# A hybrid decoder block on one Trainium2 core: two PSUM accumulation banks in place of four

## Chip, core and metric

The kernel runs on one core of one Trainium2 chip. The metric is the device time of one execution in microseconds (us), taken as the median of several runs. Profiles are of one execution, taken by the hardware profiler.

## What is computed

One decoder layer over 16 meta tokens and 256 input tokens (272 rows of 1024 numbers), in float32. Cut to what matters:

```
a = rmsnorm(h, g_mix);  proj = a @ w_in            # split into q k v qi ki wi cu cb cc ga gb
y_attn = sparse_attention(q, k, v, qi, ki, wi) @ w_attn_out     # 8 heads, best 68 keys per query
y_conv = (cb * conv3(cc * cu)) @ w_conv_out
h = h + (sigmoid(ga) * y_attn + sigmoid(gb) * y_conv) @ w_out
f = rmsnorm(h, g_ffn)
h = h + (silu(f @ w_gate) * (f @ w_up)) @ w_down   # width 2816
out = rmsnorm(h, g_final)[16:]
```

## The kernel before, in words

**Units.** All weights are cut into 158 tiles of 128 x 1024 numbers, listed in `UNITS` (`unit_order`, lines 49 to 63). A tile holds, for 128 output columns, the eight blocks of 128 x 128 that contract with the 1024 inputs. A unit is the work of one such tile: eight steps of three float32r products each (high weight times high activation, high times low, low times high), summed in one PSUM bank. `narrow` (line 218) writes 24 matmuls of 256 to 272 columns (lines 214 to 216). `product` (line 255) takes the high and the low activation side by side in one matmul of 512 columns (line 250) and adds one of 256 columns for the low weight (line 253), so its bank holds two halves that `total` (line 243) adds up, with a copy on ACT (line 245) and an addition on DVE (line 246).

**Order of the units.** Four `qi`, three early gates, `ki`; then for eight blocks `cc`, `cu`, `cb`; for eight heads `k`, `q`, `v`; then gates, `co` and `ao` (output projections of the two branches), `wo`, and 22 pairs `gate`, `up` of the FFN. The down projection has eight long sums of 22 blocks each. The order is written out by hand (`manual_schedule`): every engine works through its instructions in the order in which the program issues them.

**What stands around a unit.** `step` (line 434) first calls `ahead(i)`, which issues the splitting of coming weights: ACT rounds a tile to its high part (line 137), DVE subtracts to get the low part (line 145), and SP fetches the next tile into a ring of seven. `ahead` ends with `flush`, which issues the DVE subtractions put off by `split` (lines 118 to 124): the low half of an activation. After that come the unit's matmuls, and then the instructions that read its bank. So a subtraction that `split` puts off reaches DVE only in the next unit's call.

**Heads.** Right behind the matmuls of unit `k`, `behind(j, 0)` issues the attention of head j-2 (`attend`, lines 427 to 431), the logits and softmax of head j-1 (`logits`) and the transposes of v of head j-1 (`values`). Then `split` copies k to its high part on ACT and puts off `k_lo` (line 120), which reads the same bank. Unit `q` follows, then unit `v`.

**Start.** The first units are issued by hand (lines 574 to 601): after each unit's matmuls the one before it is read, by `indexer_queries` (ACT line 294, DVE line 296) or `early_gate` (DVE line 571), behind one or two weight splits. Between them the row sums are turned into inverse norms on POOL (line 201), spread by transposes (line 207) and applied (ACT, POOL and DVE lines 564 to 566). `ki` is read by `indexer_keys` (last at line 281).

**FFN.** The first `gate` unit's bank is kept until the inverse norms `rstd` are there: its `total` is issued behind `final_rms`, the first `up` unit and the copy of `rstd`. `final_rms` (line 625) multiplies the squares with a column of ones (line 191), which gives row sums in two banks.

**Banks.** PSUM has two pools: `acc` for the units (`bank`, line 88) and `misc` for all else (`side`, line 91), four banks each, handed out in rotation. A unit's first matmul waits until the last reader of the bank's former tile has ended.

Of the kernel before, what the change touches and what calls it, by code (L numbers as in the profile page):

```python
# [68 lines left out]
def program(nc, tc, h_in, params, weights, out):  # L69
    ctx = ExitStack()  # L70
# [5 lines left out]
    raws = pool("raws", RAW)  # L76
    his = pool("his", HIS)
    los = pool("los", LOS)
    acc = ctx.enter_context(tc.tile_pool(name="acc", bufs=4, space=bass.MemoryType.PSUM))
    misc = ctx.enter_context(tc.tile_pool(name="misc", bufs=4, space=bass.MemoryType.PSUM))  # L80
    ctx.enter_context(tc.manual_schedule())

# [35 lines left out]
    def split(hi, lo, src, now=False):  # L118
        act(hi, src, AF.Copy)  # L119
        low = lambda: V.tensor_sub(lo, src, hi.bitcast(F32))  # L120
        if now:
            low()
        else:
            pending.append(low)
# [25 lines left out]
    def ahead(i):  # L150
        split_to(i + 1 + AHEAD)
        high_to(i + 2 + AHEAD)
        flush()
# [31 lines left out]
    B = [(0, P), (P, P)]  # L185

    def token_sums(parts, groups, where=bank):
        o = [where() for _ in groups]
        for i, sq in enumerate(parts):
            for t, (c0, n) in enumerate(groups):  # L190
                mm(o[t][0:n, 0:1], sq[:, c0:c0 + n], ones, start=i == 0, stop=i == len(parts) - 1)
        return o

    def inverse_rms(o, groups):
        r = ring.tile([P, 3], F32, name="rt")
        if len(groups) == 3:
            V.memset(r[:, 0:1], 1.0)
        for t, (c0, n) in enumerate(groups):
            V.tensor_scalar(r[0:n, t:t + 1], o[t][0:n, 0:1], 1.0 / D, EPS, op0=OP.mult, op1=OP.add)
        r = r[:, 0:len(groups)]  # L200
        G.tensor_tensor(r, r, half[:, 0:len(groups)], OP.pow)  # L201
        return r

    def spread(r, groups):
        o = side()
        for i, (c0, n) in enumerate(groups):
            nc.tensor.transpose(o[:, c0:c0 + n], r[0:n, i:i + 1].to_broadcast([n, P]), ident[0:n, 0:n])
        return o
# [34 lines left out]
    def total(o):  # L243
        t = temp(S)
        act(t, o[:, S:2 * S], AF.Copy)  # L245
        V.tensor_tensor(t, o[:, 0:S], t, OP.add)  # L246
        return t
# [7 lines left out]
    def product(i, src, c0=0):  # L255
        o = bank()
        hi, lo = got.pop(i)
        w = lambda k: slice(k * P, k * P + P)
        for k in range(KT - 1):
            wide_high(o, hi[:, w(k)], src, k, c0, start=k == 0, stop=False)  # L260
            wide_low(o, lo[:, w(k)], src, k, c0, start=False, stop=False)
        k = KT - 1
        wide_low(o, lo[:, w(k)], src, k, c0, start=False, stop=False)
        wide_high(o, hi[:, w(k)], src, k, c0, start=False, stop=True)
        return o
# [321 lines left out]
    r = inverse_rms(token_sums(sums, ALL, side), ALL)  # L587
# [25 lines left out]
    sq_sum = one.tile([P, S], F32, name="sq_sum")  # L613

    def squares(j, h):
        if j == 0:
            act(sq_sum, h, AF.Square)
        else:
            sq = temp(S)
            act(sq, h, AF.Square)  # L620
            if j == KT - 1:
                return sq
            G.tensor_tensor(sq_sum, sq_sum, sq, OP.add)  # L623

    def final_rms():
        return inverse_rms(token_sums([sq_sum, sq_last], B), B)

    for j in range(KT):
        i = first["wo"] + j
# [9 lines left out]
        sq_last = squares(j, h)  # L639
# [4 lines left out]
    for j in range(NF):  # L644
        i = first["gate"] + 2 * j
        ahead(i)
        og = product(i, fT)
        if j == 0:
            r = final_rms()
            ahead(i + 1)  # L650
            ou = product(i + 1, fT)
            act(rstd, spread(r, B)[:, 0:S], AF.Copy)
        s = total(og)
        V.tensor_tensor(s, s, rstd, OP.mult)
        act(s, s, AF.Silu)  # L655
        G.tensor_tensor(s, s, rstd, OP.mult)  # L656
        if j:
            ahead(i + 1)
            ou = product(i + 1, fT)
        V.tensor_tensor(s, s, total(ou), OP.mult)  # L660
        split(gu[j // KT].hi[:, j % KT], gu[j // KT].lo[:, j % KT], s)

    for j in range(KT):
# [21 lines left out]
        sq_last = squares(j, h)  # L685
# [3 lines left out]
    def turn_out(k):  # L689
        for t in range(2):  # L690
            c = (k % 4) * P
            nc.tensor.transpose(tps[t][k // 4][:, c:c + P], hT[:, k, t * P:t * P + P], ident)

    for k in range(4):
        turn_out(k)
    r = final_rms()
    for k in range(4, KT):
        turn_out(k)
    y_out = one.tile([P, 2, D], F32, name="big0")
# [56 lines left out]
```

## Time and profile before

| what | value |
|---|---|
| median of 3 runs | 504.36 us (504.21 to 505.34) |
| profiled execution, span from first to last instruction | 502.3 us |
| profiled execution, its own time besides the span | not given |
| TensorE (PE) busy | 492.7 us, 98% |
| weight loads (PEld) | 444.5 us, 88% |
| VectorE (DVE) busy | 362.7 us, 72% |
| ScalarE (ACT) busy | 301.9 us, 60% |
| GpSimd (POOL) busy | 73.3 us, 15% |
| DMA, weights queue | 51.6% of 16 engines |

The engines' busy times are shares of the same span and overlap. The start of an instruction and its duration give its end; "[idle before <-releaser]" behind a row is how long the engine stood idle before it and which instruction ended that.

### The profile page before, as it was taken

The numbers are of one execution on the slowest core, as the hardware profiler recorded it, in microseconds if no ns is written. First come the engines' busy times: TensorE is split into PE (matmuls) and PEld (weight loads), VectorE is DVE, ScalarE is ACT, GpSimd is POOL, SyncE is SP. The second block draws the span as 40 slices with busy tenths as digits, with TensorE's granted clock in tenths as the row PEclk, the third lists the DMA queues.
The fourth block names the chain that finished last, engine by engine and source line by source line (L and its number), as shares of the span: only waits on it lengthen the run. The fifth ranks groups of instructions, "written<-read, shape, count | busy, mean of one in ns | idle before, by whom it ended". The sixth has DMA issues, their size and how long they took to land.

```text
span 502.3 us, 8349 instructions
## 1 busy us (share of the span) xinstructions
PE 492.7 (98%) x3157; PEld 444.5 (88%) x3157; DVE 362.7 (72%) x661; ACT 301.9 (60%) x567; POOL 73.3 (15%) x75
## 2 busy tenths in 40 slices
PE   8999999999999999999999999999999999999995
PEld 6988889999999999888888989888888888888895
DVE  5898678886677777587776797778777777764521
ACT  6685566655577777765656465666666656553511
POOL 3451112211000000000000012121221122000110
PEclk9999999999999999999999999999999999999999
DMA  8847335556434544365556475456656565665002
GB/s 311 322 129 251 127 127 185 193 169 215 163 127 127 159 135 133 124 204 197 182 176 201 133 246 176 155 187 201 203 178 197 173 196 182 206 204 177 1 0 85
DMA packets 24376, 86.09 MB, mean 171 GB/s; under 512 B 2832, under 2 KB 2832, under 8 KB 24336
## 3 DMA queue, kind: packets, MB, share of 16 engines
q1 hardware_dynamic: 24192, 85.54, 51.6%
q8 instruction: 25, 0.41, 0.3%
q14 instruction: 15, 0.12, 0.1%
q10 hardware_dynamic: 144, 0.02, 0.0%
HBM read 84.50 MB, written 1.05 MB: 170 GB/s over the span
## 4 chain that ended last, share of the span: by engine, by line
PE 90%; issue 3%; DVE 2%; ACT 1%; DMA 1%; POOL 1%; SPq 0%; POOLq 0%; DVEq 0%
PE acc L250 42%; PE acc L253 21%; PE acc L214 7%; PE acc L215 7%; PE acc L216 7%; DMA h_all<-in_h_in_dram 1%; PE misc L304 1%; DVE aT L566 1%; PE misc L303 1%; PE misc L410 1%; ACT temp L555 0%; PE misc L427 0%; PE misc L216 0%; POOL rt L201 0%; PE misc L214 0%
## 5 line engine op out<-in xcount | busy, mean ns | idle before, releaser
L250 PE MATMUL acc<-aT,whi 128*128 128x512 f32 x576 | 202.7, 399 | 0.0
L145 DVE TENSOR_TENSOR wlo<-raw,whi 128x1024 fp32r<-128x1024 f32 x158 | 192.8, 1225 | 7.0 <-ACT whi L137 4.8
L137 ACT ACTIVATE whi<-raw 128x1024 fp32r<-128x1024 f32 x158 | 163.8, 1047 | 0.4 <-PE acc L250 0.3
L253 PE MATMUL acc<-aT,wlo 128*128 128x256 f32 x576 | 150.1, 281 | 0.0
L250 PEld LDWEIGHTS acc<-aT,whi 128*128 128x128 f32 x576 | 105.3, 188 | 19.7
L250 PE MATMUL acc<-big,whi 128*128 128x512 f32 x330 | 115.2, 394 | 0.0
L253 PEld LDWEIGHTS acc<-aT,wlo 128*128 128x128 f32 x576 | 108.8, 189 | 5.7
L253 PE MATMUL acc<-big,wlo 128*128 128x256 f32 x330 | 88.4, 282 | 0.0
L215 PE MATMUL acc<-aT,whi 128*128 128x272 f32 (+2 forms) x272 | 78.1, 287 | 1.1 <-DVE aT L566 1.1
L214 PE MATMUL acc<-aT,whi 128*128 128x272 f32 (+2 forms) x272 | 78.6, 289 | 0.0
L216 PE MATMUL acc<-aT,wlo 128*128 128x272 f32 (+2 forms) x272 | 77.6, 285 | 0.0
L246 DVE TENSOR_TENSOR temp<-acc,temp 128x256 f32<-128x256 f32 x87 | 36.9, 424 | 49.8 <-ACT temp L245 49.8
L250 PEld LDWEIGHTS acc<-big,whi 128*128 128x128 f32 x330 | 60.6, 188 | 11.9
L253 PEld LDWEIGHTS acc<-big,wlo 128*128 128x128 f32 x330 | 62.0, 188 | 2.5
L215 PEld LDWEIGHTS acc<-aT,whi 128*128 128x128 f32 x272 | 51.3, 189 | 1.8 <-DVE aT L566 1.3
L214 PEld LDWEIGHTS acc<-aT,whi 128*128 128x128 f32 x272 | 51.4, 189 | 0.7
L216 PEld LDWEIGHTS acc<-aT,wlo 128*128 128x128 f32 x272 | 51.2, 188 | 0.0
L119 ACT ACTIVATE big<-temp 128x256 fp32r<-128x256 f32 x45 | 18.8, 418 | 47.0 <-DVE temp L660 23.2
L623 POOL TENSOR_TENSOR sq_sum<-sq_sum,temp 128x256 f32<-128x256 f32 x12 | 11.0, 918 | 236.6 <-ACT temp L620 236.6
L245 ACT ACTIVATE temp<-acc 128x256 f32<-128x256 f32 x87 | 32.7, 376 | 13.9 <-PE acc L250 11.5
L656 POOL TENSOR_TENSOR temp<-temp,rstd 128x256 f32<-128x256 f32 x22 | 26.0, 1182 | 93.9 <-ACT temp L655 93.9
L239 DVE TENSOR_TENSOR h_all<-h_all,acc 128x256 f32<-128x256 f32 x16 | 6.7, 416 | 28.6 <-PE acc L250 21.7
(162 smaller groups left out, 529.5 us busy)
## 6 DMA issues: line engine op xcount, KB each, us to landing
raw<-in_weights_dram SPq DMA_DIRECT2D x158, 512.0 KB, 3.5
h_all<-in_h_in_dram SPq DMA_DIRECT2D x4, 272.0 KB, 4.6
out_dram<-big SPq DMA_DIRECT2D x4, 256.0 KB, 2.3
raw<-in_weights_dram SPq DMA_DIRECT2D x2, 256.0 KB, 3.8
par<-in_params_dram ACTq DMA_DIRECT2D x1, 24.0 KB, 3.3
```

What stands on the lines that cost most here:

```text
L119: act(hi, src, AF.Copy)
L137: act(high[i], raw[i], AF.Copy)
L145: V.tensor_sub(lo, raw.pop(i), high[i].bitcast(F32))
L214: mm(o, wh, xh, start=first, stop=False)
L215: mm(o, wh, xl, start=False, stop=False)
L216: mm(o, wl, xh, start=False, stop=last)
L245: act(t, o[:, S:2 * S], AF.Copy)
L246: V.tensor_tensor(t, o[:, 0:S], t, OP.add)
L250: mm(halves(o), w, src.both[:, k, :, c0:c0 + S], **kw)
L253: mm(o[:, 0:S], w, src.hi[:, k, c0:c0 + S], **kw)
L623: G.tensor_tensor(sq_sum, sq_sum, sq, OP.add)
L656: G.tensor_tensor(s, s, rstd, OP.mult)
```

## The change

The pool `acc` gets two banks instead of four. The two row sums of the FFN take banks from `misc` (`side`), because the first gate's bank is still held when they are made; the last row sums keep the main banks, because all four side banks hold transposes by then.

```diff
-    acc = ctx.enter_context(tc.tile_pool(name="acc", bufs=4, space=bass.MemoryType.PSUM))
+    acc = ctx.enter_context(tc.tile_pool(name="acc", bufs=2, space=bass.MemoryType.PSUM))
...
-    def final_rms():
-        return inverse_rms(token_sums([sq_sum, sq_last], B), B)
+    def final_rms(where):
+        return inverse_rms(token_sums([sq_sum, sq_last], B, where), B)
...
         if j == 0:
-            r = final_rms()
+            r = final_rms(side)
...
     for k in range(4):
         turn_out(k)
-    r = final_rms()
+    r = final_rms(bank)
```

No instruction changes its place on any engine; the tiles' banks and the waits at the units' first matmuls change. On TensorE, at the end of a head's unit `q` and the start of its unit `v`, whose first matmul is the row of line 214 (the third to last of these rows; "waits" names the engines whose counters it waits for):

```order
 L253 MATMUL acc<-aT,wlo 128x256 x2
 L250 MATMUL acc<-aT,whi 128x512
-L214 MATMUL acc<-aT,whi 128x272
+L214 MATMUL acc<-aT,whi 128x272 [waits DVE_49]
 L215 MATMUL acc<-aT,whi 128x272
 L216 MATMUL acc<-aT,wlo 128x272
```

The first matmul of `v` waited for nothing before; now it waits for DVE. The reader it waits for stands in this part of DVE's queue, which is the same in both kernels, here for head 7 (`acc_2541` is the bank of its unit `k`, `misc_2566` the attention of head 5, `misc_2576` the logits and `misc_2591` the values of head 6):

```order
L246 TENSOR_TENSOR temp_2572<-misc_2566,temp_2572 128x256 [waits Activation_49]
L377 ISA p_2583,mx_2584<-misc_2576,bias_121 128x144 [waits PE_49]
L377 ISA mx_2584 128x1
L377 ISA p_2583,mx_2584<-misc_2576,bias_121 128x272
L377 ISA mx_2584 128x1
L378 TENSOR_SCALAR mx_2584<-mx_2584 128x2 [waits DVE_49]
L145 TENSOR_TENSOR wlo_2603<-raw_2233,whi_2537 128x1024 [waits DMAHW0_49]
L120 TENSOR_TENSOR big1_1816<-temp_2572,big1_1816 128x256 [waits Activation_49]
L120 TENSOR_TENSOR v_lo_2596<-misc_2591,v_hi_2595 128x256 [waits PE_49,Activation_49]
L403 TENSOR_TENSOR vm0_479<-misc_2591,vm0_479 16x128
L120 TENSOR_TENSOR k_lo_2601<-acc_2541,k_hi_2600 128x272 [waits Activation_49]
```

Nothing moved here: `k_lo` still stands last of eleven rows that begin with the attention issued behind unit `k`. On TensorE at the FFN's second gate (`acc_3893`; `acc_3854` is the first `up`, `misc_3871` the spread inverse norms), before:

```order
L250 MATMUL acc_3854<-aT_3566,whi_3689 128x512
L207 MATMUL misc_3871<-ident_114,rt_3844 128x128 [waits Pool_49]
L207 MATMUL misc_3871<-ident_114,rt_3844 128x128 [waits DVE_49]
L250 MATMUL acc_3893<-aT_3566,whi_3719 128x512
L253 MATMUL acc_3893<-aT_3566,wlo_3745 128x256
```

and with the change:

```order
L250 MATMUL acc_3854<-aT_3566,whi_3689 128x512
L207 MATMUL misc_3871<-ident_114,rt_3844 128x128 [waits Pool_49]
L207 MATMUL misc_3871<-ident_114,rt_3844 128x128 [waits DVE_49]
L250 MATMUL acc_3893<-aT_3566,whi_3719 128x512 [waits DVE_49,PE_49]
L253 MATMUL acc_3893<-aT_3566,wlo_3745 128x256
```

The second gate's first matmul, which waited for nothing, now waits for DVE, which reads the first gate's bank.

## Rows read from the trace of the kernel before

**Rows 1.** Page, busy us (share of the span) x instructions:

```profile
PE 492.7 (98%) x3157; PEld 444.5 (88%) x3157; DVE 362.7 (72%) x661; ACT 301.9 (60%) x567; POOL 73.3 (15%) x75
```

**Rows 2.** Page, chain that ended last, share of the span by engine:

```profile
PE 90%; issue 3%; DVE 2%; ACT 1%; DMA 1%; POOL 1%; SPq 0%; POOLq 0%; DVEq 0%
```

**Rows 3.** TensorE's waits, longest first: us in total, times, longest:

```profile
PE acc L182 <- POOL temp L156: 1.1, 1, 1.1
```

**Rows 4.** Stretches: us, busy us (instructions) by engine, granted clock, DMA share, GB/s:

```profile
30.00:42.00 12.00, 10.91 (x88) 10.46 (x86) 11.91 (x19) 8.24 (x12) 1.79 (x2) 1.00 0.61 194
...
118.00:206.00 88.00, 88.00 (x657) 84.29 (x657) 63.42 (x151) 60.18 (x142) 0.00 (x0) 1.00 0.47 150
...
320.00:490.00 170.00, 170.00 (x978) 148.67 (x977) 115.77 (x177) 93.47 (x155) 31.77 (x27) 1.00 0.51 164
```

**Rows 5.** Timeline of PE, 18 to 39 us: start us, duration us, instruction, [idle before]:

```profile
18.69 0.37 PE L214 MATMUL acc<-big,whi 128*128 128x256 f32 x1
...
22.21 0.59 PE L207 MATMUL misc<-ident,rt 16*128 16x16 f32 x3 [0.40 <-POOL rt L201]
...
31.18 0.29 PE L214 MATMUL acc<-aT,whi 128*128 128x272 f32 x1
31.31 0.29 PE L215 MATMUL acc<-aT,whi 128*128 128x272 f32 x1
...
34.44 0.39 PE L215 MATMUL acc<-aT,whi 128*128 128x272 f32 x1 [1.09 <-DVE aT L566]
34.67 0.30 PE L216 MATMUL acc<-aT,wlo 128*128 128x272 f32 x1
...
38.49 0.28 PE L214 MATMUL acc<-aT,whi 128*128 128x258 f32 x1
```

**Rows 6.** Timeline of DVE, 18 to 40 us:

```profile
18.93 0.86 DVE L296 TENSOR_TENSOR big<-acc,big 64x256 fp32r<-64x256 f32 x2
...
33.56 0.41 DVE L571 TENSOR_TENSOR gate<-acc,rstd 128x256 f32<-128x256 f32 x1
...
39.75 0.42 DVE L281 SCALAR_TENSOR_TENSOR temp<-acc,rstd 8x256 f32<-8x256 f32 x1
```

**Rows 7.** Timeline of POOL, 20 us:

```profile
20.26 1.90 POOL L201 TENSOR_TENSOR rt<-rt,half 128x3 f32<-128x3 f32 x1 [4.47 <-DVE rt L199]
```

**Rows 8.** Timeline of PE: first matmuls of v (heads 0, 1, 7), ga1, gates 1, 2:

```profile
119.96 0.29 PE L214 MATMUL acc<-aT,whi 128*128 128x272 f32 x1
...
129.80 0.29 PE L214 MATMUL acc<-aT,whi 128*128 128x272 f32 x1
...
196.34 0.29 PE L214 MATMUL acc<-aT,whi 128*128 128x272 f32 x1
...
210.04 0.40 PE L250 MATMUL acc<-aT,whi 128*128 128x512 f32 x1
...
313.47 0.48 PE L250 MATMUL acc<-aT,whi 128*128 128x512 f32 x1
...
318.96 0.63 PE L250 MATMUL acc<-aT,whi 128*128 128x512 f32 x2
```

**Rows 9.** Timeline of DVE: last readers of the banks two units ahead:

```profile
119.68 0.43 DVE L120 TENSOR_TENSOR k_lo<-acc,k_hi 128x272 fp32r<-128x272 f32 x1
...
130.28 0.44 DVE L120 TENSOR_TENSOR k_lo<-acc,k_hi 128x272 fp32r<-128x272 f32 x1
...
193.12 0.42 DVE L246 TENSOR_TENSOR temp<-misc,temp 128x256 f32<-128x256 f32 x1 [2.34 <-ACT temp L245]
...
196.86 0.44 DVE L120 TENSOR_TENSOR k_lo<-acc,k_hi 128x272 fp32r<-128x272 f32 x1
...
210.62 0.42 DVE L246 TENSOR_TENSOR temp<-acc,temp 128x256 f32<-128x256 f32 x1
...
314.44 0.43 DVE L246 TENSOR_TENSOR temp<-acc,temp 128x256 f32<-128x256 f32 x1 [2.54 <-ACT temp L245]
...
319.46 0.42 DVE L246 TENSOR_TENSOR temp<-acc,temp 128x256 f32<-128x256 f32 x1 [0.23 <-ACT temp L245]
```

## The prediction

> **What bounds the kernel now.** I read the busy times first: TensorE is busy for 492.7 us of a span of 502.3 us [rows 1], and the chain of work that ended last is TensorE for 90% [rows 2]. Next the list of TensorE's waits: it has five lines of one wait each, the longest 1.1 us, together 3.7 us, all before 35 us [rows 3, 5]. From 118 to 206 us, the attention stage, TensorE is busy for 88.00 of 88.00 us, and from 320 to 490 us for 170.00 of 170.00, at the full granted clock [rows 4]. So TensorE's stream is the time: whatever makes it wait after 42 us is added whole, because no gap behind it can take the delay back. The other engines run beside it, and their lag is free as long as nobody on TensorE waits for it. That lag is what the change puts a price on.
>
> **The change part by part.** Matmuls, copies and transfers stay as many and in the same order on each queue, SP's and POOL's too. Only two things move: which bank a tile gets, and so what a unit's first matmul waits for. With two banks, unit n needs the last reader of unit n-2. I went through all units of the trace and compared the start of each unit's first matmul with the end of the last read of the unit two ahead. Most have 1 to 2.5 us to spare. Where the reader ends later, the difference is the price. Two small amounts come on top. The release takes about 0.05 us: POOL's power ends at 22.16 us and the transpose that needs it starts at 22.21 [rows 5, 7]. And the restart costs about 0.1 us: without a wait the second matmul of a unit starts 0.13 us after the first (31.18 and 31.31), after the existing wait at 34.44 it starts 0.23 us after it (34.67) [rows 5], since the weights could not be loaded ahead.
>
> *Start, up to 42 us.* The indexer queries qi1 and qi3 meet first. qi3's first matmul starts at 18.69 [rows 5]; qi1's last reader, the second of two DVE subtractions, ends at 18.93 + 0.86 = 19.79 [rows 6]. qi3 starts 1.15 us later, 1.25 with the restart. The transposes of the row norms at 22.21 now wait 0.40 us for POOL [rows 5], which absorbs that much, so they and all of the norm's consumers on ACT, POOL and DVE shift by some 0.8 us. With that shift the unit ki has to wait for the gate unit two ahead: 33.56 + 0.41 + 0.8 + 0.05 = 34.8 against 31.18 [rows 5, 6], 3.7 us late. Inside ki the wait of 1.1 us for aT goes away [rows 5], leaving some 2.6. The next meeting, cu0 with ki, agrees: its last reader ends at 39.75 + 0.42 + 0.8 + 0.05 = 41.0 against 38.49 [rows 5, 6], 2.5 late, 2.6 with the restart. I take **2.6 us**; the ends are 1.7 (the readers do not shift at all: 40.22 - 38.49) and 3.8 (nothing is absorbed).
>
> *Attention.* Units run k, q, v for each head, so v waits for k's bank. k is read twice: by ACT, and by a DVE subtraction that is queued until the q unit's call, behind the previous head's softmax work, a weight split, and v's two subtractions. For head 7 that subtraction ends at 196.86 + 0.44 = 197.30, and v's first matmul starts at 196.34; for head 1 it is 130.72 against 129.80 [rows 8, 9]. With release: 1.01 and 0.97 us. Heads 2 to 6 lie between 0.98 and 1.06. Does it repeat, or does the first wait buy the rest? It repeats: the DVE run ahead of k_lo begins each time with an idle of 2.34 us [rows 9], so DVE is not behind; it waits for the matmuls that stand right behind k, and a later k makes it later by as much. Seven times (1.01 + 0.1) is 7.8 us. Head 0 has no such work: 119.68 + 0.43 + 0.05 against 119.96 is 0.2, with restart 0.3 [rows 8, 9]. **8.1 us**; ends 7.2 (no restart cost) and 9.4 (each wait of heads 1 to 7 longer by 0.2 us, half the subtraction's own 0.44).
>
> *First gates.* ga1 waits for gb0, whose sum ends on DVE at 210.62 + 0.42 = 211.04; ga1 starts at 210.04 [rows 8, 9]: 1.05 plus the restart, **1.15 us**. co0 just ahead waits for ga0 by a part of the same time and adds nothing beyond it.
>
> *FFN, row sums.* Four matmuls of one column and two DVE reads change their bank only: nothing. But the first gate's result is held until the row norms are there: its sum ends at 314.44 + 0.43 = 314.87, and gate 1 starts at 313.47 [rows 8, 9]: 1.45 plus 0.1, **1.55 us**. In the units that follow the readers are late too: gate 1 is read until 319.46 + 0.42 = 319.88, while gate 2 starts at 319.59 - 0.40 = 319.19 [rows 8, 9], the rows' end less one matmul. That is 0.69 late, but the 1.55 us already lost put gate 2 behind it, if the readers' backlog stays where it is. If it moves with TensorE, 2 us more are due here: that is the upper end.
>
> *Everything else* has time to spare: the projections of the convolution stage, the output projections (a reader at the closest ends 0.6 us early) and the down projection, where a bank is held for 8 us. The last row sums use the two main banks, whose readers must have finished anyway for the sums to exist: nothing.
>
> Sum: 2.6 + 8.1 + 1.15 + 1.55 = 13.4 us. The profiled span of 502.3 becomes 515.7. The page gives no time of that execution besides its span; the runs' median is 504.36, 2.1 us above it, and I carry these 2.1 over: **517.8 us**. Measurements of this kernel tell 0.2% (1 us) from no change, as its runs spread from 504.21 to 505.34.
>
> **The clock.** TensorE has paused here before without losing its clock: around the 1.1 us wait at 34 us the granted clock is 1.00, the 2.4 GHz level, for the whole stretch from 30 to 42 us [rows 4, 5]. The Trainium skill, "TensorE: Matmul & The Clock Gate", section "A second HAM failure mode: psum-queue depth-cycling", tells of a kernel that cycled through PSUM banks, paused often between groups of matmuls and kept falling to the lower clock. By that rule the pauses of the attention stage would each cost more than themselves. The row speaks against it; as a rival it gets a price below.
>
> **The rivals.**
> *The backlog moves along (FFN).* Gate 1's delay shifts ACT and DVE as well, and the next units wait again, 0.7 us and falling. For it: each unit's readers start from its own last matmul. Against: the backlog comes from one table load and the norms, which the delay does not repeat. 519.8 us.
> *Part of the waits is absorbed.* If k_lo's DVE work moves forward once TensorE stalls (weight splits ahead of it done earlier), the heads fall from 1.1 to some 0.5 us: 4 us less, 513.8. Against: the idle of 2.34 us ahead of that work [rows 9].
> *The clock falls.* If each v unit of seven heads ran at 1.2 GHz, each would take its 24 spacings of 0.13 us twice, 3.1 us more: 517.8 + 21.8 = 539.6. The row at 34 us is against it. By the rule of the Trainium skill above it would be this case.
> *Not slower.* The lost 13 us come back in the FFN if the supply of weights sets the pace there: while TensorE waits, the DMA and the splits would run up to seven tiles ahead, and later units would run faster. It decides from the point at which 66 units could each give back 0.2 us. Then 504.4. Against it: TensorE shows no wait at all after 35 us and is busy 170.00 of 170.00 us [rows 3, 4]; a full stream has nothing to give back.
> *The change does nothing.* If no unit's start were tied to the last reader of the unit two ahead, 504.4 too. The order of the built kernel shows those waits where there were none.
>
> **How the numbers follow.** Forecast as summed 0.74; backlog moving 0.11; partly absorbed 0.09; clock 0.03; not slower 0.02; nothing done 0.01. The forecast's own ends are 1.7 + 7.2 + 1.05 + 1.45 = 11.4, so 515.8, and 3.8 + 9.4 + 1.2 + 3.6 = 18.0, so 522.4, if all err the same way. The range of 515.0 to 521.0 takes in the low end, the moving backlog and most of the high end. It leaves out the clock, no change, and the lower part of the absorbed case. Slower by over 0.2%: all cases but the last two, 0.97. These two make 0.03, of which I give 0.02 to within 0.2% and 0.01 to faster, since stages that get weights early could only gain by small amounts.
>
> **What would show it.** In the changed kernel's list of TensorE's waits there should be new lines: for k_lo eight times, about 1.0 us each and 0.2 for head 0; for the sum at L246 at ga1, co0 and gate 1, together some 2.6; for L296, L571 and L281 before 45 us. TensorE's busy time stays near 492 us while the span grows, the attention stage from 88 to some 96 us, the stage of 320 to 490 us keeps its length, and the granted clock stays 1.00. Wrong would be: attention waits that shrink from head to head, a stage at a lower clock, or waits that go on through the FFN.

## The result, and the profile after

The changed kernel takes 518.38 us (median of 4 runs, 517.72 to 518.66). The kernel before, run beside it on the same chip, takes 504.85 us (4 runs, 504.21 to 505.34). The ratio is 1.027, with a 95% interval of 1.0252 to 1.0288. The profiled execution took 517.72 us and has a span of 515.9 us, 13.6 us more than the span before.

The page of the changed kernel, busy time by engine and the chain that ended last by engine, to be read beside [rows 1, 2]:

```profile
PE 496.9 (96%) x3157; PEld 444.9 (86%) x3157; DVE 363.9 (71%) x661; ACT 303.2 (59%) x567; POOL 73.3 (14%) x75
```

```profile
PE 83%; DVE 6%; ACT 5%; issue 3%; DMA 1%; SPq 0%; POOL 0%; POOLq 0%; DVEq 0%; ACTq 0%
```

Every engine does as many instructions as before, in nearly the same busy time. What is new is that the chain leaves TensorE: DVE and ACT have 11% of it, where they had 3%. The waits of TensorE in the changed kernel (us in total, times, longest) say which work of theirs it is:

```profile
PE acc L214 <- DVE k_lo L120: 6.1, 7, 0.9
PE acc L250 <- DVE temp L246: 1.9, 2, 1.3
PE acc L214 <- DVE big L296: 1.5, 2, 1.3
PE acc L227 <- DVE big L546: 1.2, 1, 1.2
PE acc L182 <- POOL temp L156: 1.1, 1, 1.1
PE acc L214 <- DVE gate L571: 1.0, 2, 0.8
PE acc L214 <- DVE rt L197: 0.2, 1, 0.2
```

The lines for L546 and L182 wait for data and not for a bank (the wait for POOL is that of [rows 3]). The others are the forecast waits: `k_lo` in the heads, the sum at L246 at the gates, and L296 and L571 at the start; L197 is a memset of 0.06 us right behind a read at L296. Two forecast lines are missing, L281 and an eighth `k_lo`: cu0 and v0 do start later, but TensorE's records of the matmuls ahead of them cover the 0.2 to 0.3 us.

Busy time by stage, with borders shifted by the delay so far, so that each stretch holds the same work as before (us, then busy us and instructions of PE, PEld, DVE, ACT, POOL, then the granted clock, DMA share and GB/s):

```profile
44.56:120.56 76.00, 76.00 (x527) 69.61 (x527) 60.04 (x135) 46.53 (x91) 17.33 (x18) 1.00 0.49 163
120.56:217.05 96.49, 90.33 (x658) 84.43 (x657) 64.12 (x151) 60.25 (x142) 0.00 (x0) 1.00 0.42 137
...
333.65:503.65 170.00, 170.00 (x978) 148.60 (x977) 114.29 (x175) 93.29 (x154) 31.12 (x27) 1.00 0.49 161
```

The convolution stage and the FFN hold the matmuls of before in the same time, 170.00 us for the FFN as in [rows 4]. The attention stage needs 96.49 us for what took 88.00 us [rows 4]; 0.08 of them are a late second matmul of cu0, which the shift of 2.56 us leaves out. Of the 8.41 us that are left TensorE stands idle for 6.16 us. The other 2.25 us, some 0.3 at each of the eight waits, count as busy: a matmul is recorded with 0.29 us although the next one usually starts 0.13 us after it [rows 5], so the last one before a wait covers part of it, and the first one behind it is drawn out.

TensorE's rows at the places of the forecast (start us, duration us, instruction, idle before): qi3, the transposes, ki and cu0 of the start; v0, v1 with its second matmul, v7; co0, ga1, gate 1:

```profile
19.96 0.36 PE L214 MATMUL acc<-big,whi 128*128 128x256 f32 x1 [0.17 <-DVE rt L197]
...
22.98 0.59 PE L207 MATMUL misc<-ident,rt 16*128 16x16 f32 x3
...
34.85 0.36 PE L214 MATMUL acc<-aT,whi 128*128 128x272 f32 x1 [0.21 <-DVE gate L571]
...
41.05 0.36 PE L214 MATMUL acc<-aT,whi 128*128 128x258 f32 x1
...
122.79 0.39 PE L214 MATMUL acc<-aT,whi 128*128 128x272 f32 x1
...
133.75 0.39 PE L214 MATMUL acc<-aT,whi 128*128 128x272 f32 x1 [0.83 <-DVE k_lo L120]
133.98 0.29 PE L215 MATMUL acc<-aT,whi 128*128 128x272 f32 x1
...
207.29 0.39 PE L214 MATMUL acc<-aT,whi 128*128 128x272 f32 x1 [0.87 <-DVE k_lo L120]
...
219.04 0.47 PE L250 MATMUL acc<-big,whi 128*128 128x512 f32 x1 [0.58 <-DVE temp L246]
...
222.16 0.50 PE L250 MATMUL acc<-aT,whi 128*128 128x512 f32 x1
...
327.13 0.47 PE L250 MATMUL acc<-aT,whi 128*128 128x512 f32 x1 [1.30 <-DVE temp L246]
```

And the readers that they wait for, on DVE:

```profile
18.96 0.86 DVE L296 TENSOR_TENSOR big<-acc,big 64x256 fp32r<-64x256 f32 x2
...
40.49 0.42 DVE L281 SCALAR_TENSOR_TENSOR temp<-acc,rstd 8x256 f32<-8x256 f32 x1
...
133.26 0.44 DVE L120 TENSOR_TENSOR k_lo<-acc,k_hi 128x272 fp32r<-128x272 f32 x1
...
203.04 0.42 DVE L246 TENSOR_TENSOR temp<-misc,temp 128x256 f32<-128x256 f32 x1 [2.70 <-ACT temp L245]
...
206.80 0.44 DVE L120 TENSOR_TENSOR k_lo<-acc,k_hi 128x272 fp32r<-128x272 f32 x1
...
326.56 0.42 DVE L246 TENSOR_TENSOR temp<-acc,temp 128x256 f32<-128x256 f32 x1 [2.54 <-ACT temp L245]
...
331.58 0.42 DVE L246 TENSOR_TENSOR temp<-acc,temp 128x256 f32<-128x256 f32 x1 [0.23 <-ACT temp L245]
```

Laid against the rows of before, these give the delay of TensorE from place to place:

| place | start before, us [rows 5, 8] | start after, us | delay, us |
|---|---|---|---|
| cu0 | 38.49 | 41.05 | 2.56 |
| v0 | 119.96 | 122.79 | 2.83 |
| v1 | 129.80 | 133.75 | 3.95 |
| v7 | 196.34 | 207.29 | 10.95 |
| ga1 | 210.04 | 222.16 | 12.12 |
| gate 1 | 313.47 | 327.13 | 13.66 |

From v1 to v7 each head adds 7.00 / 6 = 1.17 us, and nothing is added behind gate 1. The table is read at first matmuls. Where the second one comes late too (the restart), 0.08 us follow at cu0 and some 0.1 at each v and at ga1; the 0.1 of ga1 is gone again at 229 us, in the last products of the attention.

### The profile page after: what moved, and what is told of

The parts are those of the page before. It is cut to its first block, busy times and chain, and to the rows that moved or that the text cites. A ratio compares the mean times of both kernels' runs of the same rounds, so it can differ in the third digit from the quotient of the medians.

```text
span 515.9 us, 8360 instructions
## 1 busy us (share of the span) xinstructions
PE 496.9 (96%) x3157; PEld 444.9 (86%) x3157; DVE 363.9 (71%) x661; ACT 303.2 (59%) x567; POOL 73.3 (14%) x75
## 4 chain that ended last, share of the span: by engine, by line
PE 83%; DVE 6%; ACT 5%; issue 3%; DMA 1%; SPq 0%; POOL 0%; POOLq 0%; DVEq 0%; ACTq 0%
PE acc L250 38%; PE acc L253 19%; PE acc L214 8%; PE acc L215 7%; PE acc L216 7%; ACT p L381 1%; DMA h_all<-in_h_in_dram 1%; DVE p L377 1%; PE misc L304 1%; DVE temp L246 1%; DVE wlo L145 1%; ACT whi L137 1%; DVE aT L566 1%; ACT temp L245 1%; DVE v_lo L120 1%
## 5 line engine op out<-in xcount | busy, mean ns | idle before, releaser
L246 DVE TENSOR_TENSOR temp<-acc,temp 128x256 f32<-128x256 f32 x87 | 36.9, 424 | 52.4 <-ACT temp L245 52.4
```

## The experiments

**Late readers** is the theory of the prediction: a unit's first matmul waits for the last read of the unit two ahead, and each wait costs the lag of that read and a restart of some 0.1 us. **Shared depth** is the first rival: the smaller number of banks costs time in itself, spread over the units, so that each bank taken away costs a part and an earlier read helps little. **Slower stream** is the second: matmuls or reads run slower in the changed banks, the row sums' side banks among them.

**Three banks.** One number of the changed kernel:

```diff
-    acc = ctx.enter_context(tc.tile_pool(name="acc", bufs=2, space=bass.MemoryType.PSUM))
+    acc = ctx.enter_context(tc.tile_pool(name="acc", bufs=3, space=bass.MemoryType.PSUM))
```

> The changed kernel with three accumulation banks instead of two, all else as changed. Late readers (my theory): a unit waits for the last reader of the unit three ahead. In the trace of before no such reader ends later than the first matmul it would hold, by at least 0.3 us, so all of the 13.4 to 13.7 us comes back: 504.4 to 505.5 us, and TensorE's wait list is that of before. Shared depth (rival: ACT and DVE run behind, and each bank less costs in proportion): about half of the loss stays, some 511 us. Slower stream (rival: matmuls run slower when fewer banks alternate): between the two, with TensorE's mean matmul times above those of before.

Measured: 504.08 us (10 runs) beside 504.39 (13 runs), ratio 0.9994 (0.9985 to 1.0003). TensorE's waits are five lines, all before 42 us, and none is for a bank. So the time does not fall bank by bank. With three banks a unit waits for the read three ahead, which has a whole unit more, 24 matmuls of 0.125 us [rows 5]; a reader 1 us late is then 2 us early. This speaks against shared depth.

**Row sums in side banks, four main banks.** The change's second part alone, which also stands in the three kernels further down that keep four banks:

```diff
         if j == 0:
-            r = final_rms()
+            r = final_rms(side)
```

> Four accumulation banks as before, and only the FFN's row sums moved to side banks, the other part of the change done alone. My theory: no effect, a span of 502.3 us within 0.5 us. Rival: the row sums in side banks hold up the transposes behind them, which take side banks too: the first FFN units up to 1 us later.

Measured: 504.91 us in one run, span 503.1 us, and no new wait of TensorE. The 0.8 us over the profile of before arise at 10 to 13 us, far ahead of the row sums, where TensorE's clock fell in this execution (the last section): it is 0.84 us late at 23 us and still so at the end. The row sums cost nothing.

**k read first, two banks.** In the changed kernel, the copy and the subtraction of k are issued ahead of the attention of the head before, and the subtraction is not put off:

```diff
             o = narrow(i, aT)
-            behind(j, 0)
             k = Pair(two, [P, L], "k")
-            split(k.hi, k.lo, o)
+            split(k.hi, k.lo, o, now=True)
+            behind(j, 0)
```

> The changed kernel (two banks), with unit k's two readers (the copy on ACT and the subtraction on DVE) issued right behind k's matmuls, ahead of the attention, logits and values of the heads before, and the subtraction not put off. Late readers: the eight waits of unit v for k_lo vanish, 8.5 us of the 13.7: a span of 507.4 us and 509.9 us in time; the waits at the start, at the first gates and at the FFN stay as they are. Shared depth: v's wait is replaced by waits of q, v or k for other readers in the same stage, and under 3 us come back: 515 us or more.

Measured: 509.01 us (4 runs, 508.63 to 509.5), ratio to the kernel before 1.0092 (1.0075 to 1.0109); span 506.8 us. All waits for `k_lo` are gone, and the attention stage (us and columns as in the stages above) holds its 657 matmuls in the former time:

```profile
120.50:208.50 88.00, 88.00 (x657) 84.20 (x656) 63.55 (x150) 60.92 (x143) 0.00 (x0) 1.00 0.45 150
```

All of the attention stage's 8.4 us come back from the order of k's reads, with two banks. The time is 0.9 us below the forecast of 509.9, of which 0.55 us lie at the start, which the edit does not touch (cu0 came 2.02 us later than before, not 2.56). This is the strongest evidence for late readers, and the one that shared depth and a slower stream cannot give. A slower stream is also refuted by the changed kernel itself, whose 978 matmuls of the FFN take 170.00 us with two banks as with four.

**First FFN gate read first, two banks.** The sum of the first gate is issued ahead of the row norms, not behind them:

```diff
         og = product(i, fT)
+        s = total(og)
...
-        s = total(og)
```

> The changed kernel (two banks), with the first FFN gate's sum issued right behind its matmuls, ahead of the row norms. Late readers: the wait of gate 1, 1.4 us, vanishes. The readers of the next units, 0.7 us late in the trace of before, are then met for the first time, less the 0.4 us that the earlier sum takes off ACT's and DVE's queues: gate 2 waits some 0.3 to 0.5 us, and the span becomes 514.9 us. If the readers' backlog were only a matter of that one sum, the full 1.4 us come back: 514.5 us. Shared depth: the waits of the next units together take all of it back: 515.9 us.

Measured: 517.25 us in one run, span 515.5 us. Gate 1's delay of 1.54 us is gone, and two small ones take its place, 0.37 us at the up unit behind it and 0.19 at gate 2, so some 1.0 us is saved, as expected. The span hides it, because in this execution TensorE's clock fell at 11 us and the start ended 0.6 us later.

**Start's reads first, two banks.** In the start, each read is issued ahead of the weight splits that stood before it (four such places):

```diff
-    split_to(3)
     indexer_queries(last, 0)
+    split_to(3)
...
-        split_to(i + 3)
...
             early_gate(last, i - 1)
+        split_to(i + 3)
```

> The changed kernel (two banks), with the readers of the first units (indexer queries and early gates) issued ahead of the weight splits that stood before them, at the start only. Late readers: the waits of qi2, qi3 and of the gate units and ki for those readers vanish or shrink, and 1.5 to 2.6 us of the start's 2.6 come back: the matmuls of cu0 start 0 to 1.1 us later than before instead of 2.6. Shared depth: what the readers gain, the splits lose; TensorE waits for the low parts of the weights instead, and nothing comes back (2.6 us or more at cu0).

Measured: 517.03 us in one run, span 515.3 us. cu0 starts at 40.39 us, 1.90 us later than before and not 2.56, so only 0.66 us came back, a miss: 1.5 to 2.6 were expected. The reason is on DVE and at cu0 on TensorE:

```profile
35.53 3.48 DVE L145 TENSOR_TENSOR wlo<-raw,whi 128x1024 fp32r<-128x1024 f32 x3
...
39.82 0.42 DVE L281 SCALAR_TENSOR_TENSOR temp<-acc,rstd 8x256 f32<-8x256 f32 x1
```

```profile
40.39 0.36 PE L214 MATMUL acc<-aT,whi 128*128 128x258 f32 x1 [1.21 <-DVE temp L281]
```

The waits for the queries (1.7 us, L296 and L197) are gone, but those for the gates grew from 1.0 to 1.4 us, and the read of ki still stands behind three splits of 3.48 us together and became the new last one. A chain of late readers gives back only what its latest leaves. The rival that expects the splits to lose what the reads gain has a part here as well: in qi2 TensorE waits 0.3 us for a weight's low half (`wlo`), which it did not before.

**k, first gates and FFN gate read first, two banks.** The edits of the third and fourth experiment, and for the first gates:

```diff
             o = product(i, aT, META)
+            t = total(o)
...
-            t = total(o)
             act(t, t, AF.Sigmoid)
```

> The changed kernel (two banks) with the readers of unit k, of the gates ga0, ga1 and gb1, and of the first FFN gate all issued right behind their matmuls. Late readers: the savings add up, since each place has its own: of 13.7 us of delay only the start's 2.6 and the 0.4 us in the FFN that the run with the early first gate showed stay, 3.0 in all: 507.4 us in time (1.006 of before). Shared depth: new waits between the places, so that 5 us or more stay: 509.5 us or more.

Measured: 507.39 us (4 runs, 507.08 to 507.7), ratio 1.0056 (1.0043 to 1.0069); span 505.6 us. The remaining 3.33 us of delay are 2.59 at the start, 0.37 at ga1 and 0.37 at the first up unit, each with its restart. The savings add up, as late readers has it.

**Norms on DVE, four banks.** A try at the start: two of the norm's products go from POOL to DVE, so that aT comes earlier:

```diff
+    early_t = {k: temp(L) for k in (0, 1)}
+    for k, t in early_t.items():
+        V.tensor_tensor(t, h_all[:, k], rstd, OP.mult)
```

> Four banks as before (row sums in side banks), and the products of the first two row blocks with the inverse norms at the start taken from POOL to DVE, which stands idle for 1.9 us there in the trace of before. An attempt at a faster kernel: TensorE's wait for aT inside ki, 1.1 us, shrinks or vanishes, because POOL's chain of eight products becomes six. 503.3 us, 0.998 of before. If DVE's own splits are what ki and the gate units need, nothing changes: 504.4 us.

Measured: 504.75 us (12 runs, 503.25 to 506.41), ratio 1.0002 (0.999 to 1.0014). No gain that can be measured, where 503.3 was expected: TensorE's wait for aT inside ki is 1.0 us still, at the same matmul. POOL is through with its products at 30.4 us (31.8 before), but DVE's part of the blocks, at 34.5 us, stands behind a weight split and a gate as before. A miss.

**k read later, two banks.** The opposite of the third experiment, to see whether a later read is absorbed: one more product on DVE (its result is not used) ahead of `k_lo` in every head of the changed kernel:

```diff
             k = Pair(two, [P, L], "k")
+            t = temp(L)
+            pending.append(lambda: V.tensor_tensor(t, h_all[:, 0], h_all[:, 1], OP.mult))
             split(k.hi, k.lo, o)
```

> The changed kernel (two banks) with one more DVE instruction of some 0.43 us (a product of 272 columns that nobody reads) put ahead of k_lo in each of the eight heads: the suspected cost made larger. Late readers: unit v waits that much longer in each head, eight times 0.43 us: the span grows by 3.4 us to 519.3 us, and each wait for k_lo from 0.9 to 1.3 us. Shared depth or a backlog that is paid once: DVE is idle for 29% of the span and takes it in, under 1 us: 516.9 us or less.

Measured: 519.83 us in one run, span 518.1 us (519.3 forecast). The waits for `k_lo` grow to 8.7 us in 8, the longest from 0.9 to 1.2 us, and each head is 0.33 us longer. The direction is that of late readers and nothing is absorbed; the size is below the 0.43 us forecast. DVE's rows around it:

```profile
133.12 0.44 DVE L465 TENSOR_TENSOR temp<-h_all 128x272 f32<-128x272 f32 x1
133.48 0.43 DVE L120 TENSOR_TENSOR k_lo<-acc,k_hi 128x272 fp32r<-128x272 f32 x1
```

The instruction is recorded with 0.44 us, but the next one starts 0.36 us after it. Neighbours on DVE overlap by nearly 0.1 us, so an extra one costs its spacing and not its duration.

**Two banks, mended.** All the reads above first, and the read of ki ahead of its splits:

```diff
-        if not final:
+        if not final and kind != "ki":
             ahead(i)
         if kind == "ki":
             keep["wi"] = indexer_keys(narrow(i, aT))
+            ahead(i)
```

> Two banks, with every late reader moved ahead: those of unit k, of the gates, of the first FFN gate, of the first units (as in the run with the start's reads first), and those of ki ahead of the three weight splits that stood before them. Late readers: of the 13.7 us only about 0.5 us at the start (ki's wait for its own inputs comes later) and 0.4 in the FFN stay: 505.0 to 505.6 us, 1.002 of before. Shared depth: 507 us or more.

Measured: 506.22 us (5 runs, 505.79 to 506.95), ratio 1.0036 (1.0022 to 1.005), somewhat above the forecast. The waits for banks left are 1.4 us in two for the early gates (at this kernel's line 572) and 0.2 us at L246; in its profile the clock fell as in the second experiment, for 1.2 us. The forecast lacked a price of the cure: the splits that now stand behind the read of ki come late themselves, and cu0 waits for its weight's low half (0.3 us idle, 0.6 us later).

**A filled start, four banks.** Since several profiles had shown that fall of the clock behind TensorE's gaps at 5.5 to 9.3 us, three idle products (nothing reads them) were put into the gaps, with the norms on DVE as above:

```diff
+    idle = side()
+
+    def busy():
+        mm(idle[:, 0:S], wide[:, 0:P], wide, start=True, stop=True)
...
+                if i == 0 and k == 4:
+                    busy()
                 mm(o, hi[:, w(k)], xh, start=k == 0, stop=False)
+                if i == 0 and k in (0, 4):
+                    busy()
```

> Four banks, row sums in side banks, the two products of the norms on DVE, and three idle matmuls put into TensorE's gaps between 5.7 and 9.3 us, whose result nobody reads. In the profiles with the row sums in side banks and with the norms on DVE the granted clock fell to its lower level from 9.9 to 13.3 us, behind those gaps, and the first units came about 1 us later. If the gaps are the reason, the clock stays up in every run, the runs spread less (under 0.8 us from lowest to highest instead of 1.5), and with the 0.6 us that the products gave the median is 503.3 us, 0.998 of before. If not, the spread stays and the idle matmuls cost up to 0.5 us.

Measured: 503.94 us (12 runs, 503.54 to 504.62) beside 504.63 (18 runs, 503.4 to 505.6), ratio 0.999 (0.998 to 1.0). The runs spread over 1.1 us, not the 0.8 forecast, beside 2.2 for the kernel before; the 503.3 us, which counted on a gain from the norms, were not reached.

**The fill alone, four banks.** The same without the norms on DVE (the row sums are in side banks here too, which costs nothing, as shown; the products have 256 columns and take two matmuls each):

> The kernel before (four banks) with nothing changed but three idle matmuls of 272 columns in TensorE's gaps between 5.7 and 9.3 us. Filled gaps (the gaps of 5.5 to 9.3 us are what the fall of the clock at 10 us follows): clock 1.00 from 6.8 us on, runs within 1.2 us of each other, median 503.9, ratio 0.9985 to 0.9995. Rival, norms or side banks did it in the run before: clock falls to 0.5 from about 10 to 13 us in some runs, spread 2 us, median 504.6, ratio 1.000.

Measured: 503.96 us (11 runs, 503.65 to 504.34) beside 504.69 (21 runs, 503.71 to 505.54), ratio 0.9989 (0.998 to 0.9998). The fill does it, not the norms.

**Two banks, mended and filled.** The mended kernel with the norms on DVE and the fill:

> Two banks, all reads moved ahead, the norms on DVE, and the same idle matmuls. Late readers: the mended two-bank kernel's 506.2 less some 0.7 for the clock and 0.4 for the norms: 505.1, between 504.5 and 505.8, so 0.1% above before. Shared depth (fewer banks cost something that no late reader explains): 1 us or more above that, 506.2 or over.

Measured: 505.36 us (11 runs, 505.17 to 505.87), ratio 1.0014 (1.0005 to 1.0023), where late readers had it. Two banks with early reads stand 0.14% above the kernel before; all but 0.67 of the changed kernel's 13.5 us are gone, though the fill brings part of that. It is 1.40 us above the filled four-bank kernel of the experiment before, and 1.42 above the one with the norms on DVE too. Laid matmul by matmul against the profile of the latter, it ends 1.35 us later, and three places give that: 0.37 us at ga1 and 0.37 at the first up unit, as with the reads of k and the gates first, and 0.60 us at cu0, which is no wait for a bank:

```profile
39.11 0.39 PE L221 MATMUL acc<-aT,wlo 128*128 128x258 f32 x1 [0.34 <-DVE wlo L145]
```

The wait of 0.8 us for an early gate, also in its profile, adds nothing, as ki then finds its aT ready. So what two banks still cost is a late read twice and a late weight split once, and no remainder is left for shared depth. None of the kernels was measurably faster than the fill with four banks.

## Why the prediction was right

The time (517.8 forecast, 518.38 measured) and the span (515.7 forecast, 515.9 measured) agree for the reason given: lags of single readers, each added whole. That the places agree to 0.1 us is in part luck: the two small amounts were each wrong by about 0.1 us at several of them, and cancelled. The release is 0.05 us behind `k_lo` and at ga1, as forecast, but 0.14 us at the start (19.82 to 19.96 at qi3, 40.91 to 41.05 at cu0) and 0.15 at co0 and gate 1 (326.98 to 327.13). Why it differs is not shown.

*Start: 2.6 forecast, 2.64 measured,* 2.56 at cu0's first matmul and 0.08 of restart. The readers moved by 0.74 us instead of 0.8, and the longer release made up for it. The points on the way agree as well: qi3 1.27 us late (1.25 forecast), the transposes 0.77 (0.8), ki 3.67 (3.7), and inside ki 2.50 (2.6). One row differs: qi2 was already 0.89 us late. Some 0.55 of it came from `big` at L546, which was later in this execution, and 0.34 from a wait for a bank that the forecast passed over: qi2 meets qi0's read before qi3 meets qi1's. It did not matter, as qi3 waits for a read that ends at 18.96 + 0.86 = 19.82 us, against 19.79 before [rows 6]: a fixed end swallows a delay ahead of it. At qi3 the restart was not due (0.37 us for the first matmul before, 0.36 now: it stands behind the row sums), and the release was longer by as much.

*Attention: 8.1 forecast; v0 0.30 and v1 to v7 8.12 measured, 8.42 together.* Seven heads at 1.11 were forecast and they took 1.12 to 1.21 us. The release is 0.05 us: `k_lo` ends at 133.26 + 0.44 = 133.70, v1 starts at 133.75. The restart is 0.1 us: the second matmul starts 0.23 us after the first instead of 0.13. The step "it repeats" holds, and the rival of part of the waits absorbed fell: the waits do not shrink from head to head, and the run of DVE work ahead of `k_lo` still begins with DVE idle, 2.70 us where it was 2.34 [rows 9]. `k_lo` itself ends 2.98 us later than before in head 1 and 9.94 in head 7, as late as TensorE is ahead of those waits (2.96 and 9.92).

*First gates: 1.15 forecast, 1.18 measured.* co0 took 0.76 of it first (219.04 against 207.23 before), and ga1 the rest. That co0 adds nothing beyond the same time was right.

*Gate 1: 1.55 forecast, 1.54 measured.* Here too two errors cancel. The restart was not due. Gate 1's first matmul had 0.48 us before too [rows 8], because it stood behind the transposes; it has 0.47 now. So "plus 0.1" was wrong for a place where the stream was already broken, and the release took 0.15 us instead of 0.05. With the 0.1 us of ga1's restart given back in between, 2.64 + 8.42 + 1.18 - 0.11 + 1.54 make the 13.66 us of the table. The backlog stayed where it was: the sums of the first gate and of gate 1 moved from 314.44 and 319.46 [rows 9] to 326.56 and 331.58, both by 12.12 us, while TensorE moved by 13.66 at gate 1. The second of them then ends at 332.00 us, 0.8 us before gate 2 starts, and the rival of the moving backlog fell.

*The clock.* It is 1.00 through the attention stage with its seven waits of up to 0.9 us, as in the rows above, so the clock added nothing to any of them. The Trainium skill ("TensorE: Matmul & The Clock Gate", section "A second HAM failure mode: psum-queue depth-cycling") tells of a kernel whose pauses between groups made the clock fall again and again; this case does not show it.

*Not slower, and nothing done,* fell with the new waits, and with the FFN's 170.00 us for the same 978 matmuls: nothing was given back there.

*What the text had wrong besides:* "TensorE's busy time stays near 492 us". It is 496.9 us, because the records of matmuls cover part of each wait, as the attention stage showed. For that reason the lines of waits sum to less than the delay, which is better read from the starts of matching instructions.

The miss with the start's reads has one root. Where several late readers follow each other, as at the start, I took each one's lag from the old trace as what its removal gives back; the next reader then became the last.

## What to carry to other kernels

Price a cut in banks by comparing, unit by unit, the end of the last read with the start of the unit that will need the bank, with 0.05 to 0.15 us for the release and 0.1 us for a weight stream that the wait newly breaks; add it whole where the waiting engine has no idle time behind. Before giving banks away, look at what stands ahead of the last reader in its engine's queue: here one subtraction put off behind the neighbour's softmax cost 8.4 us, and issuing k's reads first gave them back. But what stood ahead of the reader is then later itself: at cu0 a weight split moved behind the read of ki cost 0.6 us. The Trainium skill ("Perfetto Trace Analysis", section "Optimization Strategy") says that a gap that keeps repeating on the engine that should be saturated can mean too few buffers. The trace agrees: the seven waits for `k_lo`, 0.8 to 0.9 us each, were that. An earlier read cured them as well as a third bank did.

## What the chip showed that I had not expected

TensorE's clock falls at the start in some executions of the same program. In the profile of the second experiment (four banks) the granted clock, the third number from the end of each line, is at the lower level of 1.2 GHz from 11 to 13 us:

```profile
5.00:9.00 4.00, 3.16 (x13) 2.31 (x12) 2.91 (x6) 2.89 (x8) 2.12 (x2) 1.00 0.98 340
9.00:11.00 2.00, 1.64 (x8) 1.51 (x9) 1.49 (x4) 2.00 (x6) 0.02 (x1) 0.74 1.02 416
11.00:13.00 2.00, 2.00 (x11) 2.00 (x11) 1.89 (x2) 1.77 (x5) 1.16 (x1) 0.50 1.03 420
13.00:15.00 2.00, 2.00 (x18) 2.00 (x17) 1.96 (x4) 1.96 (x7) 0.42 (x1) 0.91 1.02 414
```

From 11 to 13 us TensorE does 11 matmuls there; with the fill alone it does 19, at the full clock:

```profile
5.00:9.00 4.00, 3.81 (x19) 2.81 (x18) 2.92 (x6) 2.56 (x7) 1.91 (x2) 1.00 1.01 367
9.00:11.00 2.00, 1.98 (x12) 1.57 (x12) 1.27 (x4) 2.00 (x5) 0.00 (x0) 1.00 1.02 416
11.00:13.00 2.00, 2.00 (x19) 2.00 (x18) 1.71 (x2) 2.00 (x5) 1.02 (x1) 1.00 1.03 422
```

This goes with most of the spread between runs of the kernel before. In the last set its 21 runs fall in two groups by the mean clock of the span: ten at 0.997 or more took 503.71 to 504.45 us, eleven at 0.995 or less took 504.69 to 505.54. All 34 runs of the three filled kernels had 0.996 or more, and the medians of the two with four banks, 503.94 and 503.96, lie in the first group. So with the gaps filled the fall did not come in any run, but the gaps do not decide it alone: the profile of the kernel before has them too and kept its clock, and what tells one execution from the next stays open. The 2.1 us between span and median that the prediction carried over contain this: a run at the full clock lies 1.8 us above its span (517.72 and 515.9), so about 0.3 us is what the median run had over the profiled one; whether that was a slower start is not recorded.
